# Stick-breaking attention on one core: projection groups evacuated one step later, weight splits in halves, first output halves reloaded at an earlier place, the last pair's scores two steps further ahead

## The chip, the cores and the metric

The kernel runs on one core of a Trainium2 chip. Its engines work at the same time, each through its own queue in order: TensorE (PE) multiplies, VectorE (DVE) and ScalarE (ACT) do elementwise work, GpSimd (POOL) some more of it, and SyncE (SP) issues the DMAs. They wait for one another by semaphores. The metric is the device time of one execution in microseconds (us). Before the change it is 2205.62 us, the median of three runs (2204.3 to 2206.53).

## The reference

A trunk of two layers over 1024 positions of width 1024. Layer 0 mixes by a gated linear recurrence, layer 1 by stick-breaking attention with 16 heads of width 64; each is followed by a SwiGLU network. The change touches layer 1's mixer alone:

```
qkv = hn @ w_qkv                                  # (1024, 3*1024)
z = q @ k.T / 8                                   # for each head
strict = key index < query index
log_fail = where(strict, log_sigmoid(-z), 0)
suffix = sum of log_fail over later keys
weights = where(strict, exp(log_sigmoid(z) + suffix), 0)
o = weights @ v
out = o @ w_o
```

The kernel takes no logarithms: it forms sigmoid(-z), multiplies it up from the last key to the first with a scan, and multiplies the result with sigmoid(z).

## The kernel before, in words

Each float32 operand of a large product is held as two tiles, a rounded high part and the rest, and a product is three matmuls (`mm3`, lines 140 to 143: high by high, high by low, low by high). A split is a copy on ACT (high) and a subtraction on DVE (low).

The 16 heads are worked in eight pairs. For a pair q, `qkv_steps(q)` (line 1315) projects Q, K and V (`which` = 0, 1, 2), each in two groups of 512 positions (`n`), each group in eight steps of one `mm3`. A group's sum lies in a bank of the pool `psQ` (two banks). After the eighth `mm3` the group is evacuated: DVE multiplies the bank by the row factors into `t` (line 1337). For Q and K, ACT rounds `t` (`th`, shown as `qh_`, line 1346), DVE takes the rest (`tl`, shown as `ql_`, line 1347), and SP copies both into the layouts the scores need (`move`, line 1348: four DMAs for Q, eight for K). For V, `t` is kept and `v_turn` (line 1359) transposes it on PE four steps later, through a `psQ` bank (`vt_ps`); ACT and DVE split it into `VV` (lines 1366 and 1367). At the start of each `which` the next weights are loaded and split (`next_weights`, line 1305): one ACT copy at once, two DVE halves put on the list `later`.

The attention itself has two lists. `chunks` are blocks of scores (24 in a pair: for each head eight on the diagonal and four beside it): `z_part` multiplies on PE into a bank of `psZ` (two), `z_rest` takes two sigmoids on ACT, a scan on DVE (line 1412 on the diagonal, 1414 beside it) and a product on POOL (line 1415). `units` are blocks of keys (24 in a pair): `t_part` transposes their weights on PE into `psT` (two banks), `t_split` splits them (lines 1435 and 1436), `av_part` multiplies them with V (lines 1447 and 1448). When a head's half is complete, `gather` adds its two parts (lines 1457 and 1458), and for the second head `parts` splits the result; both go through `later`. The output halves of earlier pairs are written to DRAM (`od`, lines 1469 and 1470), because the tiles `xh` and `xl` that will hold them are still the projections' input; two halves of the last pairs go straight there.

The order of PE, ACT, DVE and POOL is that of the code, written out by hand (`manual_schedule`); SP's order is left to the framework's planner. The loop over u (line 1527) interleaves: scores eight units ahead (`LEAD`), transposes two units ahead, one task of `later`, two steps of `fill`, then `av_part` of unit u. One pass of a pair is thus 24 values of u and 48 steps of `fill`. `fill` is the projection of the pair after, and behind the last one (`all_fill`, line 1490): the reloads of the output halves, two empty steps, the last `v_turn`, the release of `psQ`, a weight split, the tile `ob` in the two banks released, two empty steps more, and then 14 `mm3` of the output projection into `ob`, one in each u. The products of the second half and what follows them (`ob_ps`) belong to the next stage.

Of the kernel before, what the change touches and what calls it, by code (L numbers as in the profile page):

```python
# [19 lines left out]
ND = D // P  # L20
NT = S // P
NB = 512
NH = S // NB
# [10 lines left out]
def trunk(  # L34
# [22 lines left out]
    nc = tc.nc  # L57
    f32 = lambda t: t.bitcast(F32)
# [40 lines left out]
    xh, xl = [None] * ND, [None] * ND  # L99
# [11 lines left out]
    def load_raw(src, shape):  # L111
        raw = rp.tile([P, D], F32, tag="raw", name="raw")
        view = raw if len(shape) == 1 else raw.rearrange("p (a b) -> p a b", a=shape[0])
        nc.sync.dma_start(view, src)
        return raw
# [11 lines left out]
    def cols(w, c0, n=P):  # L127
        return w[:, c0 : c0 + n].rearrange("(k p) c -> p k c", p=P)
# [20 lines left out]
    def wtile(nm):  # L149
        return wpool[0].tile([P, D], F32R, tag="w", name=nm)  # L150
# [91 lines left out]
    half = lambda t, n: t[:, n * NB : (n + 1) * NB]  # L242
# [1021 lines left out]
    if stage == "ffn0":  # L1264
# [7 lines left out]
    NP = HEADS // 2  # L1272
# [4 lines left out]
    od = {  # L1277
        (q, n): [dp.tile([P, NB], F32, name=f"od{x}{q}_{n}") for x in "hl"]
        for n in range(NH)
        for q in range(NP)  # L1280
        if kept(q, n)
    }

    pos = ExitStack()
    with ExitStack() as st:
# [16 lines left out]

        late, later = [], []

        def next_weights(raw):
            hi, lo = wtile("whi"), wtile("wlo")
            nc.scalar.copy(hi, raw)
            for i in range(NH):
                later.append(lambda c=half(hi, i), a=half(lo, i), b=half(raw, i): nc.vector.tensor_sub(a, b, f32(c)))
            k3 = lambda t: t.rearrange("p (k c) -> p k c", k=ND)  # L1310
            return k3(hi), k3(lo)

# [2 lines left out]
        def qkv_steps(q):  # L1315
            full = lambda tag: [ap.tile([P, S], F32R, tag=tag, name=tag, bufs=4) for _ in range(2)]
            VV[q] = ap.tile([P, NT, 2, P], F32R, tag="v", name="v", bufs=2)
            for which in range(3):
                w = wq.pop((q, which))
                nx = (q, which + 1) if which < 2 else (q + 1, 0)  # L1320
                if nx[0] < NP:
                    wq[nx] = next_weights(load_raw(cols(w_qkv, nx[1] * D + nx[0] * P), (ND,)))
                else:
                    mix[0].load(0)
                    mix[0].w[mix[0].order[0]] = next_weights(mix[0].raw.pop(0))
                    mix[0].load(1)
                    mix[0].load(2)
                for n in range(NH):
                    ps = psQ.tile([P, NB], F32, tag="qk", name="qk_ps")
                    for k in range(ND):  # L1330
                        mm3(ps, w[0][:, k], w[1][:, k], xh[k][n], xl[k][n], k == 0, k == ND - 1)
                        if k == 3 and late:
                            late.pop()()
                        if k < ND - 1:
                            yield
                    t = ap.tile([P, NB], F32, tag="t", name="t", bufs=2)
                    nc.vector.tensor_mul(t, ps, rbc[n])
                    cs = slice(n * NB, (n + 1) * NB)
                    if which == 0 and n == 0:
                        Q[q] = full("q")  # L1340
                    if which == 1 and n == 0:
                        KH[q], KL[q] = full("kh"), full("kl")
                    if which < 2:
                        th = ap.tile([P, NB], F32R, tag="qh_", name="qh_", bufs=1)
                        tl = ap.tile([P, NB], F32R, tag="ql_", name="ql_", bufs=1)
                        nc.scalar.copy(th, t)
                        nc.vector.tensor_sub(tl, t, f32(th))
                        move = lambda dst, p0, src, p1: nc.sync.dma_start(f32(dst)[p0, cs], f32(src)[p1])
                        for hx, (a, b) in enumerate(((top, bot), (bot, top))):
                            if which == 0:  # L1350
                                move(Q[q][hx], a, th, a)
                                move(Q[q][hx], b, tl, a)
                            else:
                                for dst, src in ((KH[q][hx], th), (KL[q][hx], tl)):
                                    move(dst, top, src, a)
                                    move(dst, bot, src, a)
                    else:

                        def v_turn(n=n, t=t):
                            tp = psQ.tile([P, NB], F32, tag="qk", name="vt_ps")  # L1360
                            for i in range(4):
                                nc.tensor.transpose(tp[:, i * P : (i + 1) * P], t[:, i * P : (i + 1) * P], ident)
                            src = tp.rearrange("p (b h c) -> p b h c", b=4, h=2)
                            bs = slice(4 * n, 4 * n + 4)
                            for hx in range(2):
                                nc.scalar.copy(VV[q][:, bs, hx, 0:HD], src[:, :, hx])
                                nc.vector.tensor_sub(
                                    VV[q][:, bs, hx, HD:P], src[:, :, hx], f32(VV[q])[:, bs, hx, 0:HD]
                                )

                        late.append(v_turn)
                    yield


        W = {}
# [8 lines left out]
        def z_part(q, hx, j, ci, c0, c1, diag):  # L1384
            nk = (j + 1) * P
            ps = psZ.tile([P, NB], F32, tag="z", name="z_ps")
            lhsT = Q[q][hx][:, j * P : (j + 1) * P]
            nc.tensor.matmul(ps[:, 0 : c1 - c0], lhsT=lhsT, rhs=KH[q][hx][:, c0:c1], start=True, stop=False)  # L1388
            nc.tensor.matmul(ps[:, 0 : c1 - c0], lhsT=lhsT, rhs=KL[q][hx][:, c0:c1], start=False, stop=True)  # L1389
            return ps  # L1390
# [86 lines left out]
        chunks = [c for q, hx in heads for c in chunk_list(q, hx)]  # L1477
        units = [u for q, hx in heads for u in unit_list(q, hx)]
        LEAD = 8
# [10 lines left out]
        def all_fill():  # L1490
            yield from first
            for q in range(1, NP):
                yield from qkv_steps(q)
            for q, n in od:
                nc.sync.dma_start(f32(xh[q][n]), od[q, n][0])
                nc.sync.dma_start(f32(xl[q][n]), od[q, n][1])
            yield
            yield
            late.pop()()
            qs.close()  # L1500
            mix[0].proc(1)
            po = pos.enter_context(tc.tile_pool(name="fpo", bufs=1, space=PSUM, side="right", reuse_waits="tile"))
            ob = po.tile([P, S], F32, name="ob")
            mix.append(ob)
            for _ in range(2):
                yield
            for i, d in enumerate(mix[0].order[:2]):
                w = mix[0].w[d]
                for k in range(ND - 1):
                    mm3(ob[:, i * NB : (i + 1) * NB], w[0][:, k], w[1][:, k], xh[k][0], xl[k][0], k == 0, False)  # L1510
                    yield
                    yield

        fill = all_fill()
        ready = {}
        E = mybir.EngineType
        with tc.manual_schedule(engines={E.PE, E.Activation, E.DVE, E.Pool}):
            sts, first = stats_steps(), qkv_steps(0)


            for i in range(2 * ND * NH):
                if i >= 5:
                    next(sts, None)
                next(first)
                if i >= 5 and later:
                    later.pop(0)()
            for u in range(-LEAD, len(units)):
                c = u + LEAD
                if c < len(chunks):
                    z = z_part(*chunks[c])  # L1530
                if 0 <= u + 2 < len(units):
                    ready[u + 2] = t_split(t_part(*units[u + 2]), *units[u + 2])
                if c < len(chunks):
                    z_rest(z, *chunks[c])
                if later:
                    later.pop(0)()
                for _ in range(2):
                    next(fill, None)
                if u >= 0:
                    av_part(ready.pop(u), *units[u])  # L1540
            while later:
                later.pop(0)()
# [49 lines left out]
```

## Time and profile before

| | |
|---|---|
| median of three runs | 2205.62 us |
| profiled execution, whole | 2209.81 us |
| its span, first to last instruction | 2207.9 us |
| PE busy | 2176.5 us (99%) |
| DVE busy | 1709.9 us (77%) |
| ACT busy | 1150.2 us (52%) |
| POOL busy | 287.2 us (13%) |
| mean granted TensorE clock | 0.994 |

The profile is one execution. Times in its rows count from the start of the span. A row of the timeline shows start, duration, engine, source line, the operation with the tile written and the tiles read, partitions by elements, and in brackets the idle time of the engine before it with the instruction that ended it; "issue" there means that no releaser was found. Operations overlap a little, so that the start of the next one lies up to 0.1 us before the end shown. A busy PE may still run at half clock, which the column PEclk tells.

### The profile page before, as it was taken

What the parts mean: (1) busy time and instruction counts of PE and PEld (TensorE: products, weight loads), DVE (VectorE), ACT (ScalarE), POOL (GpSimd) and SP (SyncE); (2) the same over time, 40 slices, a digit from 0 to 9 for tenths busy, and PEclk for the clock granted to TensorE, in tenths of its full rate; (3) what the DMA queues carried; (4) which work ended last, traced back from release to release, by engine and by line L of the source; (5) the groups of instructions that cost most, each with busy time, mean ns of one, the idle gap of its engine ahead of it and who ended that gap; (6) DMA issues with size and microseconds to landing.
All of it is one profiled execution on the core that took longest, in us unless ns stands there. A gap on an engine that the chain in (4) does not pass through costs nothing.

```text
span 2207.9 us, 28478 instructions
## 1 busy us (share of the span) xinstructions
PE 2176.5 (99%) x10120; PEld 1805.7 (82%) x10120; DVE 1709.9 (77%) x2383; ACT 1150.2 (52%) x2007; POOL 287.2 (13%) x379
## 2 busy tenths in 40 slices
PE   7999999999999999999999999989999999999998
PEld 6888888888888888878888888878888888888887
DVE  6887778767777887878888888876876777788876
ACT  5577435343444544546666666653533444454556
POOL 2222020000000000003334333321000000000002
PEclk9999999999999999999999999989999999999999
DMA  7111412334444764444333333532133444467442
GB/s 230 48 48 39 134 39 72 102 123 158 143 149 134 261 209 122 148 136 98 89 94 96 105 87 104 177 128 70 39 110 124 148 148 133 154 225 234 137 152 86
DMA packets 298702, 277.72 MB, mean 126 GB/s; under 512 B 16312, under 2 KB 215104, under 8 KB 298560
## 3 DMA queue, kind: packets, MB, share of 16 engines
q1 hardware_dynamic: 298544, 275.91, 40.1%
q8 instruction: 79, 1.29, 0.2%
q14 instruction: 63, 0.52, 0.1%
q10 hardware_dynamic: 16, 0.00, 0.0%
HBM read 175.71 MB, written 74.97 MB: 114 GB/s over the span
## 4 chain that ended last, share of the span: by engine, by line
PE 88%; DVE 6%; ACT 3%; DMA 1%; issue 1%; SPq 1%; DVEq 0%; ACTq 0%
PE p_ps L143 18%; PE p_ps L141 18%; PE p_ps L142 18%; PE qk_ps L143 3%; PE qk_ps L141 3%; PE qk_ps L142 3%; PE wt_ps L1426 3%; PE ob_ps L142 2%; PE ob_ps L141 2%; PE ob_ps L143 2%; PE a_ps L143 2%; PE a_ps L142 2%; PE a_ps L141 2%; PE z_ps L1388 1%; DVE F L1414 1%; PE z_ps L1389 1%
## 5 line engine op out<-in xcount | busy, mean ns | idle before, releaser
L1415 POOL TENSOR_TENSOR w<-w,F 128x128 f32<-128x128 f32 (+1 forms) x192 | 183.7, 957 | 311.1 <-DVE F L1412 159.0
L143 PE MATMUL p_ps<-vh,wcl 128*128 128x512 f32 x524 | 204.2, 390 | 0.5 <-DVE wcl L682 0.5
L143 PE MATMUL p_ps<-vh,wbl 128*128 128x512 f32 x524 | 204.4, 390 | 0.3 <-DVE wbl L672 0.2
L143 PE MATMUL p_ps<-vh,wal 128*128 128x512 f32 x524 | 204.1, 389 | 0.1
L141 PE MATMUL p_ps<-vh,wbh 128*128 128x512 f32 x524 | 204.2, 390 | 0.0
L141 PE MATMUL p_ps<-vh,wch 128*128 128x512 f32 x524 | 204.1, 389 | 0.0
L142 PE MATMUL p_ps<-vl,wbh 128*128 128x512 f32 x524 | 203.9, 389 | 0.0
L142 PE MATMUL p_ps<-vl,wch 128*128 128x512 f32 x524 | 203.9, 389 | 0.0
L141 PE MATMUL p_ps<-vh,wah 128*128 128x512 f32 x524 | 203.9, 389 | 0.0
L142 PE MATMUL p_ps<-vl,wah 128*128 128x512 f32 x524 | 203.9, 389 | 0.0
L668 ACT CAST wbh<-sb 128x1024 fp32r<-128x1024 f32 (+2 forms) x69 | 69.6, 1009 | 193.7 <-DVE sb L652 193.6
L212 POOL TENSOR_TENSOR acc<-acc,rbc 128x512 f32<-128x512 f32 x30 | 40.4, 1348 | 773.6 <-ACT rbc L211 773.6
L1436 DVE TENSOR_TENSOR tl<-wt_ps,th 128x512 fp32r<-128x512 f32 x192 | 106.0, 552 | 39.2 <-ACT th L1435 37.1
L1435 ACT CAST th<-wt_ps 128x512 fp32r<-128x512 f32 x192 | 92.5, 482 | 83.1 <-PE wt_ps L1426 82.0
L141 PE MATMUL qk_ps<-vh,whi 128*128 128x512 f32 x264 | 118.6, 449 | 0.7 <-ACT vh L215 0.7
L143 PEld LDWEIGHTS p_ps<-vh,wbl 128*128 128x128 f32 x524 | 98.3, 188 | 22.3 <-DVE wbl L672 2.0
L143 PEld LDWEIGHTS p_ps<-vh,wcl 128*128 128x128 f32 x524 | 98.4, 188 | 21.9 <-DVE wcl L682 1.6
L143 PEld LDWEIGHTS p_ps<-vh,wal 128*128 128x128 f32 x524 | 98.4, 188 | 21.3 <-DVE wal L663 1.0
L142 PEld LDWEIGHTS p_ps<-vl,wah 128*128 128x128 f32 x524 | 98.4, 188 | 20.6
L142 PEld LDWEIGHTS p_ps<-vl,wch 128*128 128x128 f32 x524 | 98.4, 188 | 20.5
L142 PEld LDWEIGHTS p_ps<-vl,wbh 128*128 128x128 f32 x524 | 98.4, 188 | 20.5
L141 PEld LDWEIGHTS p_ps<-vh,wbh 128*128 128x128 f32 x524 | 98.4, 188 | 20.3 <-ACT ta L1053 0.2
(400 smaller groups left out, 5851.2 us busy)
## 6 DMA issues: line engine op xcount, KB each, us to landing
raw<-in_ffn_w_in SPq DMA_DIRECT2D x88, 512.0 KB, 3.8
vl<-pd SPq DMA_DIRECT2D x128, 256.0 KB, 3.6
pd<-U SPq DMA_DIRECT2D x90, 256.0 KB, 2.3
raw<-in_ffn_w_out SPq DMA_DIRECT2D x56, 256.0 KB, 3.9
raw<-in_attn_w_qkv SPq DMA_DIRECT2D x24, 512.0 KB, 3.8
raw<-in_lru_w_in SPq DMA_DIRECT2D x16, 512.0 KB, 4.1
acc<-pd SPq DMA_DIRECT2D x28, 256.0 KB, 2.6
pph<-rbc SPq DMA_DIRECT2D x28, 256.0 KB, 2.5
```

Of the source, the lines that this page charges most:

```text
L141: nc.tensor.matmul(ps, lhsT=wh, rhs=mh, start=first, stop=False, **kw)
L142: nc.tensor.matmul(ps, lhsT=wh, rhs=ml, start=False, stop=False, **kw)
L143: nc.tensor.matmul(ps, lhsT=wl, rhs=mh, start=False, stop=last, **kw)
L212: (eng or nc.gpsimd).tensor_add(acc[n], acc[n], sq)
L668: nc.scalar.copy(self.full(self.wb), self.full(self.sb))
L1388: nc.tensor.matmul(ps[:, 0 : c1 - c0], lhsT=lhsT, rhs=KH[q][hx][:, c0:c1], start=True, stop=False)
L1389: nc.tensor.matmul(ps[:, 0 : c1 - c0], lhsT=lhsT, rhs=KL[q][hx][:, c0:c1], start=False, stop=True)
L1414: nc.vector.tensor_tensor_scan(rev, rev, rev, first, op0=ALU.mult, op1=ALU.bypass)
L1415: nc.gpsimd.tensor_mul(wt, wt, F[:, 1 : n + 1])
L1426: nc.tensor.transpose(tp[:, c : c + P], W[q, hx, j, kb // 4][:, (kb % 4) * P : (kb % 4 + 1) * P], ident)
L1435: nc.scalar.copy(th[:, q0:], tp[:, q0:])
L1436: nc.vector.tensor_sub(tl[:, q0:], tp[:, q0:], f32(th)[:, q0:])
```

## The change

Four edits, all in the attention stage.

- A group's last step now yields before its evacuation. `t`, `th`, `tl` and the moves are issued at the beginning of the generator's next step, ahead of the next group's first `mm3`, which is in the next u. The number of steps stays.
- `next_weights` splits in halves, as three tasks of `later`: high half 0; low half 0 and high half 1; low half 1.
- The reloads are a function, `bring_back(n)`. Those of n = 0 are issued in the last pair's V projection, once its first group has been evacuated; those of n = 1 where all were before.
- Behind the last projection the two empty steps between the making of `ob` and its first `mm3` go, so that this `mm3` follows the last `v_turn` directly. In two values of u, units 2 and 6 of the last pair (`len(units) - 22` and `- 18`), one score block more is worked in place of the two steps of `fill`. From there the scores are nine, then ten units ahead.

```diff
+        def bring_back(n):
+            for q in range(NP):
+                if (q, n) in od:
+                    nc.sync.dma_start(f32(xh[q][n]), od[q, n][0])
+                    nc.sync.dma_start(f32(xl[q][n]), od[q, n][1])
+
         def next_weights(raw):
             hi, lo = wtile("whi"), wtile("wlo")
-            nc.scalar.copy(hi, raw)
-            for i in range(NH):
-                later.append(lambda c=half(hi, i), a=half(lo, i), b=half(raw, i): nc.vector.tensor_sub(a, b, f32(c)))
+            part_hi = lambda i: nc.scalar.copy(half(hi, i), half(raw, i))
+            part_lo = lambda i: nc.vector.tensor_sub(half(lo, i), half(raw, i), f32(half(hi, i)))
+
+            def second():
+                part_lo(0)
+                part_hi(1)
+
+            later.extend((lambda: part_hi(0), second, lambda: part_lo(1)))
...
                         mm3(ps, w[0][:, k], w[1][:, k], xh[k][n], xl[k][n], k == 0, k == ND - 1)
                         if k == 3 and late:
                             late.pop()()
-                        if k < ND - 1:
-                            yield
+                        yield
                     t = ap.tile([P, NB], F32, tag="t", name="t", bufs=2)
...
                         late.append(v_turn)
-                    yield
+                        if q == NP - 1 and n == 0:
+                            bring_back(0)
...
                 yield from qkv_steps(q)
-            for q, n in od:
-                nc.sync.dma_start(f32(xh[q][n]), od[q, n][0])
-                nc.sync.dma_start(f32(xl[q][n]), od[q, n][1])
+            bring_back(1)
             yield
             yield
             late.pop()()
...
             mix.append(ob)
-            for _ in range(2):
-                yield
             for i, d in enumerate(mix[0].order[:2]):
...
+            gains = [len(units) - 22, len(units) - 18]
+            c = 0
             for u in range(-LEAD, len(units)):
-                c = u + LEAD
-                if c < len(chunks):
-                    z = z_part(*chunks[c])
+                some = chunks[c : c + 1]
+                c += 1
+                for a in some:
+                    z = z_part(*a)
                 if 0 <= u + 2 < len(units):
                     ready[u + 2] = t_split(t_part(*units[u + 2]), *units[u + 2])
-                if c < len(chunks):
-                    z_rest(z, *chunks[c])
+                for a in some:
+                    z_rest(z, *a)
                 if later:
                     later.pop(0)()
-                for _ in range(2):
-                    next(fill, None)
+                if u in gains:
+                    z_rest(z_part(*chunks[c]), *chunks[c])
+                    c += 1
+                else:
+                    for _ in range(2):
+                        next(fill, None)
                 if u >= 0:
                     av_part(ready.pop(u), *units[u])
```

## The prediction

> **What bounds the kernel now.** First the stretches of the attention stage, in a table by windows (busy time of each engine with its instruction count, granted TensorE clock, DMA share, GB/s):
>
> ```profile
> core 0: us, PE busy (x) PEld busy (x) DVE busy (x) ACT busy (x) POOL busy (x), PEclk, DMA share, GB/s
> 1120.00:1180.00 60.00, 59.63 (x319) 50.06 (x318) 50.54 (x74) 39.78 (x97) 23.45 (x39) 1.00 0.36 95
> ...
> 1435.00:1440.00 5.00, 1.09 (x7) 0.75 (x7) 4.20 (x7) 3.53 (x9) 2.45 (x2) 0.89 1.06 385
> 1440.00:1445.00 5.00, 5.00 (x16) 4.12 (x17) 3.97 (x5) 3.31 (x9) 1.09 (x1) 0.50 0.80 224
> ...
> 1470.00:1475.00 5.00, 4.40 (x16) 3.70 (x17) 3.52 (x7) 1.79 (x3) 1.09 (x1) 0.50 0.00 0
> 1475.00:1480.00 5.00, 5.00 (x24) 3.94 (x23) 1.54 (x3) 1.75 (x3) 0.00 (x0) 0.85 0.00 0
> ```
>
> A head pair takes some 60 us, TensorE (PE) is busy for 59.63 of them, and VectorE (DVE) for 50.5: inside the pairs 0.37 us each is all that can be won. More lies in the last pair: PE idle after 1435, half clock after it, half clock again at 1470. The table of waits names the places (total, times, longest):
>
> ```profile
> ACT qh__9565 L1346 <- DVE t L1337: 3.3, 1, 3.3
> PE ob L141 <- issue: 3.9, 1, 3.9
> PE z_ps L1388 <- ACT w L1409: 2.2, 6, 0.4
> ```
>
> So three sums: 2.2 us (six times) where a score waits for ACT to empty its bank, which itself waited 3.3 us for `t`; 3.9 us before `ob`; and the end. The timeline shows the second (PE rows, then DVE rows; start, duration):
>
> ```profile
> 1434.00 0.60 PE L1362 MATMUL vt_ps<-ident,t 128*128 128x128 f32 x4
> 1434.36 0.42 PE L1447 MATMUL av_ps<-th,v 128*128 128x384 f32 x1
> ...
> 1435.30 0.60 PE L1426 MATMUL wt_ps<-ident,w 128*128 128x128 f32 x4
> 1439.80 0.76 PE L141 MATMUL ob<-vh,whi 128*128 128x512 f32 x1 [3.91 <-issue]
> 1440.36 0.63 PE L142 MATMUL ob<-vl,whi 128*128 128x512 f32 x1
> ...
> 1445.97 0.39 PE L142 MATMUL ob<-vl,whi 128*128 128x512 f32 x1
> ...
> 1432.86 0.67 DVE L1337 TENSOR_TENSOR t<-qk_ps,rbc 128x512 f32<-128x512 f32 x1
> 1433.63 0.42 DVE L1436 TENSOR_TENSOR tl<-wt_ps,th 128x256 fp32r<-128x256 f32 x1
> 1434.29 1.28 DVE L1414 TENSOR_TENSOR_SCAN F<-F,F 128x512 f32<-128x512 f32 x1 [0.24 <-POOL w L1415]
> 1435.61 0.69 DVE L1458 TENSOR_TENSOR oo<-av_ps,oo 64x512 f32<-64x512 f32 x1
> ...
> 1437.84 0.66 DVE L1464 TENSOR_TENSOR vl<-oo,vh 128x512 fp32r<-128x512 f32 x1
> 1438.42 0.41 DVE L1367 TENSOR_TENSOR v<-vt_ps,v 128x256 fp32r<-128x256 f32 x1
> 1439.27 0.42 DVE L1367 TENSOR_TENSOR v<-vt_ps,v 128x256 fp32r<-128x256 f32 x1 [0.44 <-ACT v L1366]
> ...
> 1441.36 0.68 DVE L1436 TENSOR_TENSOR tl<-wt_ps,th 128x512 fp32r<-128x512 f32 x1
> ```
>
> The `[...]` of the `ob` row names no releaser, but the second `v` ends at 1439.69 and `ob` starts at 1439.80: `ob` takes the two banks of the projection pool, and the last reader of those is that `v`. I read the 3.9 us as this wait, not as the reload of outputs. The whole queue of DVE from 1434.29 to 1439.69 stands before it.
>
> **The change part by part.** Below, u counts the loop's steps from the first unit of a pair.
>
> *Evacuation a step later.* No instruction is added; `t`, `th`, `tl` and the moves of each of the 48 groups go behind the next u's `tl`, scan and popped task. (1) ACT no longer sits on `qh` when the next scores arrive, so the six score waits go: -2.2 us, and a like one of 0.3 us at the stage's start. (2) The second V group's `t` now comes after `oo`; its reader is the transpose `vt_ps`:
>
> ```profile
> 1133.61 0.69 DVE L1458 TENSOR_TENSOR oo<-av_ps,oo 64x512 f32<-64x512 f32 x1
> ...
> 1134.77 0.60 PE L1362 MATMUL vt_ps<-ident,t 128*128 128x128 f32 x4
> ```
>
> `oo` frees DVE at 1134.2 (starts of such operations lie 0.6 apart), `t` ends at 1134.87, PE starts at 1134.95 in place of 1134.77: +0.18, seven times, +1.3. (3) The K halves reach the scores over SP and DMA. The first K group of a pair in before (DVE, SP, then PE; DMA issues with their KB and us to landing last):
>
> ```profile
> 1161.39 0.67 DVE L1337 TENSOR_TENSOR t<-qk_ps,rbc 128x512 f32<-128x512 f32 x1
> ...
> 1164.88 0.66 DVE L1458 TENSOR_TENSOR oo<-av_ps,oo 64x512 f32<-64x512 f32 x1
> ...
> 1163.95 1.33 SPq L1348 DMA_DIRECT2D kl<-ql__9813  x2
> ...
> 1170.75 0.28 PE L1389 MATMUL z_ps<-kl,q 128*128 128x256 f32 x1
> ...
> kl<-ql__9813 SPq DMA_DIRECT2D x4, 128.0 KB, 2.4
> ```
>
> The second `kl` move starts at 1164.7, 3.3 us after `t`, and lands near 1167.1. In the new order `t` stands behind `oo`; with ACT free that `oo` runs at about 1163.9, `t` at 1164.5, so the move lands at 1164.5 + 3.3 + 2.4 = 1170.2, and the score needs it at 1170.75: I take nothing. Bounds per pair: 0, and the 0.5 us of slack overdrawn by as much. The second K group is needed 9 us after its `t` and has more room.
>
> *Weight splits in pieces.* ACT's 1.05 us copy (128x1024) becomes two of 0.62 us (the row of `qh`, 128x512): +0.2 us on an engine idle for 20 of 60 us. The DVE halves stay, one or two u later; weights are needed 8 u after the split begins, and the raw load that their end releases, a u later, is three tiles ahead. Zero, hidden by those u; uncovered it would be one 2.5 us step per load.
>
> *Reload sooner.* SP already issues the reloads before their place in the program:
>
> ```profile
> 1413.35 0.34 SPq L1496 DMA_DIRECT2D vl<-odl  x1
> ...
> 1420.54 0.39 SPq L1470 DMA_DIRECT2D odl<-oo  x1
> 1421.03 0.41 SPq L1495 DMA_DIRECT2D vh<-odh  x1
> ...
> 1427.78 0.32 SPq L1496 DMA_DIRECT2D vl<-odl  x1
> ```
>
> The fourteen of the first half are out by 1428, land some 5 us later, 6 us before `ob`. Moved, they gain nothing. Were some issued ahead of the last pair's second K moves, SP would hold these moves: 0 to +1.5 us (three 0.5 us issues), once; I take 0.
>
> *The last pair.* (a) `t` is now at u=0 behind scan and `oo`: 1435.61 + 0.6 = 1436.2 to 1436.9. So `vt_ps` waits from 1434.0 to 1436.95. Then `tl`, scan, `vl`, `v`, `v` follow as before, 0.4 us later: `ob` at 1440.2. (b) `ob` now stands right behind `vt_ps`, so the av, score and transposes that ran from 1434.36 to 1435.66 (1.3 us) come after it, at half clock (a product that takes 0.63 us there, as at 1440.36, and 0.39 again at 1445.97; start to start 0.43 and 0.23). The two idle stretches of 2.9 us I take to lower the clock as the 3.9 us did. DVE, which got `tl` at 1441.4, gets it at 1444.5. With the extra score at u=2, whose successor must wait 0.4 us for a bank, the second `ob` step starts at 1446.0, not 1442.99: 3.0 us behind. (c) Now the tail (PE unless marked):
>
> ```profile
> 1442.99 0.78 PE L141 MATMUL ob<-xg,whi 128*128 128x512 f32 x1
> ...
> 1468.30 0.33 PE L1426 MATMUL wt_ps<-ident,w 128*128 128x128 f32 x1 [1.09 <-DVE tl L1436]
> ...
> 1470.60 1.33 PE L1426 MATMUL wt_ps<-ident,w 128*128 128x128 f32 x4 [1.62 <-DVE tl L1436]
> ...
> 1479.03 0.39 PE L141 MATMUL ob_ps<-vh,whi 128*128 128x512 f32 x1
> ...
> 1468.16 1.97 DVE L1414 TENSOR_TENSOR_SCAN F<-F,F 128x512 f32<-128x512 f32 x1
> ```
>
> From 1442.99 to 1479.03 are 36.0 us: 2.7 idle, half of the 2.5 cold us to 1445.5 (1.2), half of the 5.9 busy cold us from 1470 to 1476.5 (2.95; the clock rows, 0.50 and then 0.85 of 5 us, put the end there) and 0.3 hidden in the slow transposes leave 28.85 of work at full clock. One score (0.23) is already done in the new order: 28.6. The scans run two steps ahead of the products, so the last of them ends by about 1469 with products still to do, and the wait for it goes. I stepped the queues on from 1446.0 with the durations of such rows (0.6 a `tl`, 0.4 to 1.7 a scan, 0.5 an ACT copy). What is late next: the score at u=7 waits 1.2 us for its bank (two scores went at u=6, and ACT reads each with two passes of 0.5), and the transposes at u=16 find PE ready at 1468.2 and their bank free at 1469.6, when the `tl` behind the last scan ends: 1.4. 1446.0 + 28.6 + 2.6 = 1477.2, against 1479.03: -1.8 us. Bounds: without any of these idle times -4.4; with half clock once more (2.95) +1.1.
>
> Sum: -0.3 - 2.2 + 1.3 - 1.8 = -3.0 us. Of the profiled execution (span 2207.9, whole time 2209.81) that makes 2206.8; it stood 4.2 us above the median 2205.62, so the forecast for the median is 2202.6, 0.14% less. About 0.2% (4.4 us) is what a measurement of this kernel tells from no change: this counts as the same.
>
> **Rules against the trace.** The rows show half clock after one idle stretch of 3.91 us, and again after two of 1.09 and 1.62 us with work between. [...]
>
> **Rivals.** *The clock holds:* both new gaps are shorter than the 3.9 us one. Then the 5.3 us from 1440.2 to 1445.5 are not halved: -2.7 more, -5.7, 2199.9. Against it stands 1470. [...] *The tail runs full:* the bank and `tl` waits (2.6) do not appear, since the scans came early: -5.6, 2200.0; for it, DVE's queue then holds less; against it, DVE is the full engine from 1460 on. Both together: -8.3, 2197.3. *Slower, the K halves come late:* each pair's first score with new keys waits. My 0.5 us of slack rests on DVE's new order; if `t` slips behind a further `tl` and scan (0.33 + 1.28) the wait is 1.1 us in each of seven pairs, +7.7: 2210.3. It decides from a wait of 1.06 us on (3.0 + 4.4 over seven); at 0.4 us the sum is zero. For it: the chain is on four engines in order, against it, the copy that ACT no longer blocks. *No effect:* the bubble costs what the lead earns (half clock in the tail too): 0, 2205.6.
>
> **How the numbers follow.** The forecast 0.42, clock holds 0.13, tail full 0.13, slower 0.20, no effect 0.12. Of the forecast's 0.42, its own range (-5 to 0) puts 0.05 beyond -4.4, and of the slower case 0.03 lies within 0.2%, of no effect 0.06 beyond +0.2%: faster 0.31, same 0.46, slower 0.23. The 8 in 10 reach from both gains together, less a little (-9), to a K wait of 0.9 us (+3.3): 2196.6 to 2208.9.
>
> **What would show it.** Right: the PE wait of scores on ACT gone from the six pairs; a PE wait before `vt_ps` of 0.1 to 0.3 us in each pair and of 3 us in the last; `ob` starting with 3 us of wait behind a second `v`; no PE wait above 1 us near the last scan; half clock around the first `ob`. Wrong: PE waits before L1389 (K late), a clock of 1.00 around `ob`, idle before `ob` that ends with a landing DMA, or a tail that goes to half clock again. The forecast fails most easily in the term -1.8, a difference between 3.0 lost and 4.8 won.

## The result and the profile after

The changed kernel takes 2211.76 us (median; 2209.74 to 2214.94) against 2206.13 us for the kernel before on the same chip (2204.3 to 2208.31). The ratio is 1.0025, 95% interval 1.0014 to 1.0036: slower by 5.6 us, where 3 us less were forecast, and above the range. The interval lies above 1, but not wholly above the 0.2% from which the forecast counts a change. Its profiled execution took 2214.94 us with a span of 2213.1.

For a single execution the span is a poor measure: the code ahead of the stage is the same in both kernels, and yet the stage's first score came anywhere from 991.1 to 994.5 in the profiles below. All kernels are therefore compared by two stretches inside the stage: the *six pairs*, from the last `vt_ps` of the first pair to that of the seventh, and the *end*, from there to the first `ob_ps`. First the rows of before that bound them, then those of after (PE rows of the timeline):

```profile
1014.59 0.60 PE L1362 MATMUL vt_ps<-ident,t 128*128 128x128 f32 x4
...
1376.38 0.60 PE L1362 MATMUL vt_ps<-ident,t 128*128 128x128 f32 x4
```

```profile
1011.91 0.60 PE L1372 MATMUL vt_ps<-ident,t 128*128 128x128 f32 x4
...
1380.46 0.66 PE L1372 MATMUL vt_ps<-ident,t 128*128 128x128 f32 x4
...
1482.94 0.40 PE L141 MATMUL ob_ps<-vh,whi 128*128 128x512 f32 x1
```

Before (its `ob_ps` row, 1479.03, stands in the prediction): 361.8 and 102.65. After: 368.55 and 102.5. The loss lies in the pairs. PE's waits there (table of waits of after: us in total, times, longest):

```profile
PE vt_ps L1372 <- DVE t L1347: 3.2, 3, 2.9
PE ob L141 <- issue: 2.6, 1, 2.6
PE z_ps L1399 <- DMA kh<-qh__12230: 1.8, 1, 1.8
PE z_ps L1399 <- ACT w L1420: 1.7, 2, 1.2
PE wt_ps L1437 <- DVE tl L1447: 1.1, 2, 0.7
PE z_ps L1400 <- DMA kl<-ql__9211: 0.6, 1, 0.6
PE z_ps L1400 <- DMA kl<-ql__10721: 0.6, 1, 0.6
```

The six waits on ACT `w` are gone, as forecast; the two left belong to the last pair. New are waits for `kl`, the moved half of K, of 0.5 to 0.6 us, one in each of the seven pairs (two are listed here). How one comes about (after; DVE, POOL, SP and PE rows):

```profile
1232.08 1.31 DVE L1423 TENSOR_TENSOR_SCAN F<-F,unit 128x128 f32<-128x128 f32 x1
1233.43 0.69 DVE L1469 TENSOR_TENSOR oo<-av_ps,oo 64x512 f32<-64x512 f32 x1
1234.13 0.69 DVE L1347 TENSOR_TENSOR t<-qk_ps,rbc 128x512 f32<-128x512 f32 x1
1235.52 0.69 DVE L1357 TENSOR_TENSOR ql__10721<-t,qh__10720 128x512 fp32r<-128x512 f32 x1 [0.69 <-ACT qh__10720 L1356]
...
1232.02 1.10 POOL L1426 TENSOR_TENSOR w<-w,F 128x512 f32<-128x512 f32 x1 [1.25 <-DVE F L1425]
...
1236.71 1.18 SPq L1358 DMA_DIRECT2D kl<-ql__10721  x2
...
1239.77 0.36 PE L1400 MATMUL z_ps<-kl,q 128*128 128x256 f32 x1 [0.61 <-DMA kl<-ql__10721]
```

This is the second K group of a pair. From `t` at 1234.13 to the product that uses the half are 5.6 us of chain: ACT, DVE, SP, landing. Before, the same operations stood so (DVE, then PE):

```profile
1171.92 0.66 DVE L1337 TENSOR_TENSOR t<-qk_ps,rbc 128x512 f32<-128x512 f32 x1
...
1180.06 0.28 PE L1389 MATMUL z_ps<-kl,q 128*128 128x256 f32 x1
```

There the chain had 8.1 us, 2.5 to spare. Against the pair's `vt_ps` (1134.77 before, 1194.40 after) `t` moved from 37.15 to 39.73: 2.6 us later. That takes the whole room, and the scores come a little earlier in the pair besides.

### The profile page after: what moved, and what is told of

Same layout as the page of the kernel before. It is cut to its first block, busy times and chain, and to the rows that moved or that the text cites. A ratio compares the mean times of both kernels' runs of the same rounds, so it can differ in the third digit from the quotient of the medians.

```text
span 2213.1 us, 28506 instructions
## 1 busy us (share of the span) xinstructions
PE 2174.9 (98%) x10120; PEld 1802.8 (81%) x10120; DVE 1728.4 (78%) x2383; ACT 1152.4 (52%) x2031; POOL 288.8 (13%) x379
## 3 DMA queue, kind: packets, MB, share of 16 engines
q8 instruction: 80, 1.31, 0.2%
## 4 chain that ended last, share of the span: by engine, by line
PE 84%; DVE 8%; ACT 3%; DMA 2%; issue 1%; SPq 1%; DVEq 0%; ACTq 0%
PE p_ps L143 18%; PE p_ps L141 18%; PE p_ps L142 18%; PE ob_ps L141 2%; PE ob_ps L142 2%; PE ob_ps L143 2%; PE qk_ps L143 2%; PE qk_ps L141 2%; PE qk_ps L142 2%; PE a_ps L143 2%; PE a_ps L142 2%; PE a_ps L141 2%; PE wt_ps L1437 2%; DVE F L1425 2%; PE z_ps L1400 1%
## 5 line engine op out<-in xcount | busy, mean ns | idle before, releaser
L1423 DVE TENSOR_TENSOR_SCAN F<-F,unit 128x128 f32<-128x128 f32 (+3 forms) x128 | 128.5, 1004 | 4.4 <-ACT F L1419 4.3
```

The source lines that it names most:

```text
L1423: nc.vector.tensor_tensor_scan(rev, rev, unit[:, NB - n :][:, ::-1], first, op0=ALU.mult, op1=ALU.add)
```

## The experiments

Theory: the late evacuation of K costs the time. Rival: the last pair's new order costs it. In the table, "six pairs" and "end" are worked out from the same three rows of each profile; the ratio is to the kernel before, timed beside it. The six pairs of before agree in both profiles, while its two ends lie 2 us apart: the end of a single profile can be off by as much.

| kernel | median us | ratio (95%) | six pairs | end |
|---|---|---|---|---|
| before, two profiles | 2206.13 | | 361.8, 361.8 | 102.65, 100.6 |
| after, five profiles | 2211.76 | 1.0025 (1.0014 to 1.0036) | 368.55, 365.2, 366.2, 365.2, 366.0 | 102.5 in all |
| evacuation alone | 2215.93 | 1.0037 (1.0024 to 1.0049) | 370.4 | 101.4 |
| change without it | 2202.53 | 0.9976 (0.9966 to 0.9987) | 357.9 | 101.3 |
| last pair's order alone | 2207.19 | 1.0001 (0.9992 to 1.0010) | 361.8 | 101.9 |
| splits alone | 2202.74 | 0.9983 (0.9975 to 0.9992) | 357.8 | 102.2 |
| change, K at once | 2205.24 | 0.9995 (0.9986 to 1.0003) | 359.9 | 103.4 |
| change, V at once | 2209.39 | 1.0016 (1.0007 to 1.0025) | 363.0 | 102.3 |
| change, fill first | 2205.12 | 0.9993 (0.9984 to 1.0002) | 359.1 | 101.05 |
| change, no POOL product | 2204.03, one run | | 359.9 | 100.15 |
| without it, V turn early | 2199.72 | 0.9971 (0.9960 to 0.9982) | 357.8 | 98.5 |
| the same, `ob` later | 2200.29 | 0.9974 (0.9964 to 0.9984) | 357.8 | 98.7 |

**The changed kernel again.** No edit.

> The changed kernel once more, nothing edited. In its first profile the 6.0 us of the span fall into: seven pairs with a wait of 0.5 to 0.6 us for the second half of K (about +0.5 us a pair over before, +3.3 by 1315), 3.5 us more in the seventh pair, where the move of the second half of K ran 2.95 us instead of 1.18, and the rest about zero. If that stretched move is a chance of one execution, the seventh pair takes 60.9 us here, not 64.3, and the span is 2209 to 2210. If it belongs to the program, the seventh pair takes 64 us again and the span is 2213. The K waits of 0.5 to 0.6 us are there in both cases.

Median 2212.79, ratio 1.0020 (1.0011 to 1.0029). The seventh pair took 60.9 us, not 64.3, and the K waits were there. So 3.4 us of the first profile came and went with one SP move; the rest stayed.

**One part alone.** The evacuation a step later, on the kernel before:

```diff
-                        if k < ND - 1:
-                            yield
+                        yield
                     t = ap.tile([P, NB], F32, tag="t", name="t", bufs=2)
...
                         late.append(v_turn)
-                    yield
```

> The kernel before with one part of the change: the projected groups evacuated a step later. Weight splits, reloads and the last pair stay as before. Theory (the evacuation costs): K waits of 0.5 to 0.6 us in each of the seven pairs as in the changed kernel, the score waits of 0.37 gone, vt waits of 0.2 to 0.3; pairs of 60.8 to 60.9 against 60.40, and some 2.9 us of a vt wait in the last pair; span 2210 to 2214, that is +2 to +6 on before. Rival (the last pair's new order costs): without it this kernel keeps before's time or better, 2204 to 2208, with pairs of at most 60.4.

And all of the change but this:

```diff
-                        yield
+                        if k < ND - 1:
+                            yield
...
                             bring_back(0)
+                    yield
```

> The changed kernel with the projected groups evacuated at once, as before; the weight splits, the reloads and the last pair stay changed. Theory (the evacuation costs): no K waits, pairs of 60.4, no vt wait of 2.9 in the last pair, and the tail of 41.6 us from the last projection to ob against 45.0 kept; span 2201 to 2205, that is -3 to -7 on before. Rival (the last pair's new order costs): 2208 or more. Weight splits in pieces, if they cost anything, show as pairs over 60.45.

And the last pair's order alone, on the kernel before:

```diff
             mix.append(ob)
-            for _ in range(2):
-                yield
...
+            gains = [len(units) - 22, len(units) - 18]
...
+                if u in gains:
+                    z_rest(z_part(*chunks[c]), *chunks[c])
+                    c += 1
```

> The kernel before with one part of the change: the last pair's scores two steps further ahead (two score blocks issued in place of fill steps, the two empty steps taken out). Theory: everything up to the last pair as before, the last pair faster by 2 to 4.8 us, span 2203 to 2206. It differs from the changed kernel without the late evacuation only by splits and reloads: if these are free, both have the same span within 0.5. Rival (the last pair's new order costs): 2208 or more.

The evacuation alone is slower than the whole change, and the change without it faster than before: the theory holds on the whole. Two things went against what I expected. First, with the evacuation alone the score waits on ACT did not go; they grew. The table of waits, then ACT and PE rows of that kernel:

```profile
PE z_ps L1386 <- ACT w L1407: 6.0, 6, 1.1
```

```profile
1237.28 0.62 ACT L1345 CAST qh__10706<-t 128x512 fp32r<-128x512 f32 x1 [3.74 <-DVE t L1336]
1237.81 1.04 ACT L1307 CAST whi<-raw 128x1024 fp32r<-128x1024 f32 x1
...
1239.62 0.50 PE L1386 MATMUL z_ps<-kh,q 128*128 128x512 f32 x1 [1.10 <-ACT w L1407]
```

The evacuation has been moved right in front of the whole-tile copy of weights, and ACT does both before it empties the next score's bank. The K waits, expected in every pair, are absent but for two, of 0.2 and 1.2 us. So this kernel is slow by the evacuation, but by another path than the changed one; that K is the path in the changed kernel rests on the experiments below. Second, the last pair's order alone is worth nothing that the times show (2207.19 against 2207.75 beside it), so the other 4.7 us between it and the change without the evacuation must come from splits or reloads, or from several parts together.

**Splits alone**, on the kernel before:

```diff
-            nc.scalar.copy(hi, raw)
-            for i in range(NH):
-                later.append(lambda c=half(hi, i), a=half(lo, i), b=half(raw, i): nc.vector.tensor_sub(a, b, f32(c)))
...
+            later.extend((lambda: part_hi(0), second, lambda: part_lo(1)))
```

> The kernel before with one part of the change: the weight splits in pieces. The changed kernel with the old evacuation has pairs of 59.65 us, the kernel before and the one with the new last pair alone 60.40; the two differ in splits and reloads. If the splits make the 0.75 us, this kernel has pairs of 59.65, no wait of scores for ACT, and a span 4.5 to 5.3 us shorter than before, 2202 to 2204. If the reloads or the two together do it, the pairs stay at 60.40 and the time at 2206 to 2208.

Six pairs of 357.8: all of it. (The reloads begin later, ahead of the eighth `vt_ps`. From the seventh to the eighth take 57.08 us here and in the change without the evacuation, and in both SP issues the first reload 36.43 us behind the seventh: moved in the code, the reloads come no earlier, and up to there they cost nothing.) PE no longer waits for ACT, and the reason is in DVE's queue. First before, then this kernel:

```profile
1142.82 0.66 DVE L1309 TENSOR_TENSOR wlo<-raw,whi 128x512 fp32r<-128x512 f32 x1
1143.40 0.68 DVE L1337 TENSOR_TENSOR t<-qk_ps,rbc 128x512 f32<-128x512 f32 x1
```

```profile
1138.64 0.66 DVE L1308 TENSOR_TENSOR wlo<-raw,whi 128x512 fp32r<-128x512 f32 x1
1139.22 0.68 DVE L1342 TENSOR_TENSOR t<-qk_ps,rbc 128x512 f32<-128x512 f32 x1
1140.59 0.69 DVE L1352 TENSOR_TENSOR ql__9575<-t,qh__9574 128x512 fp32r<-128x512 f32 x1 [0.69 <-ACT qh__9574 L1351]
...
1141.86 0.67 DVE L1308 TENSOR_TENSOR wlo<-raw,whi 128x512 fp32r<-128x512 f32 x1
```

Before, both low halves stand ahead of `t`; now the second stands behind it, a step later. Against the pair's `vt_ps` (1134.77 and 1131.43) `t` begins at 8.63 before and at 7.79 here. ACT, which waits for `t`, is free 0.84 us sooner, and the score wait of 0.37 is covered.

**Which group is late, and why.** The changed kernel with the K groups evacuated at once:

```diff
-                        yield
+                        if k < ND - 1 or not (which == 1):
+                            yield
...
+                    if which == 1:
+                        yield
```

> The changed kernel with the groups of K alone evacuated at once; those of Q and V stay a step later. Theory (the second half of K comes late because its evacuation moved): no wait of scores for K, pairs 0.7 to 0.8 us shorter than the 60.85 of the changed kernel, 60.1; the waits of vt_ps for t (0.15 to 0.31 and 2.9 in the last pair) stay. Seven pairs: 5 us off the changed kernel, 2206 to 2208. Rival (the queue of DVE is too long whatever group goes first): the wait moves to another operand and the pairs stay at 60.6 or more, 2211 or more.

The same edit with `which == 2`, the V groups:

> The changed kernel with the groups of V alone evacuated at once. Theory: the vt waits go (0.31 a pair, and 2.9 in the last pair, of which the ob wait takes back some 2.6, as where all groups go at once), the K waits of 0.5 to 0.6 stay, pairs of 60.4 to 60.55, last pair about 57.3 and the tail 44.2: together 2 to 3 us off the changed kernel, 2208 to 2210. Rival (vt waits are only the other side of the K waits): pairs stay at 60.85.

K at once takes 5.3 us off the six pairs (365.2 to 359.9), 0.88 a pair, and the waits for `kl` are gone (its long end has half clock for 13.6 us in one stretch, where the changed kernel has 6.8); V at once takes 2.2 off (0.37 a pair), and the K waits stay. Both rivals fall: the wait doesn't wander, and the two add up (5.3 + 2.2 against 365.2 - 357.9 = 7.3).

The changed kernel with `fill` ahead of the list `later`:

```diff
-                if later:
-                    later.pop(0)()
                 if u in gains:
...
                         next(fill, None)
+                if later:
+                    later.pop(0)()
```

> The changed kernel with one order turned round: within a step u the two steps of fill (and with them the late evacuation) come before the task of the list later (an oo, a low half of weights), not behind it. All evacuations stay a step late. Theory (t of K is late by its step and by the oo before it): t of the second K group comes 0.7 us earlier, the K waits of 0.5 to 0.6 fall to 0.1 or go, the vt waits of 0.15 to 0.31 go, pairs of 59.8 to 60.2, span 3 to 6 us shorter than the changed kernel's 2208.5 to 2213. Rival (only the step itself counts, 2.5 us): K waits stay at 0.5 and pairs at 60.8.

`t` now stands in front of `oo`; it begins 38.83 us behind the pair's `vt_ps` (1193.74), 0.9 sooner than after, and the K waits are gone (DVE rows of this kernel):

```profile
1231.35 1.30 DVE L1423 TENSOR_TENSOR_SCAN F<-F,unit 128x128 f32<-128x128 f32 x1
1232.57 0.66 DVE L1347 TENSOR_TENSOR t<-qk_ps,rbc 128x512 f32<-128x512 f32 x1
1233.92 0.69 DVE L1357 TENSOR_TENSOR ql__10719<-t,qh__10718 128x512 fp32r<-128x512 f32 x1 [0.69 <-ACT qh__10718 L1356]
1234.64 0.69 DVE L1469 TENSOR_TENSOR oo<-av_ps,oo 64x512 f32<-64x512 f32 x1
```

The six pairs fell by 6.1 us; the median fell with them, to a ratio to before whose interval includes 1. (The edit moves all that is on the list `later`, not `oo` alone.)

The changed kernel without POOL's product beside the diagonal:

```diff
-            nc.gpsimd.tensor_mul(wt, wt, F[:, 1 : n + 1])
+            if diag:
+                nc.gpsimd.tensor_mul(wt, wt, F[:, 1 : n + 1])
```

> The changed kernel without the product of weights and F on POOL for the score blocks beside the diagonal (so the weights of those blocks lack this factor); all else stays. Theory (the scans before the evacuation of K are held up by POOL's products): the 128x128 scan after the blocks beside the diagonal takes 0.4 us and not 1.3, the 128x512 scans 1.0 to 1.3 and not 1.8 to 2.0, t of the second K group comes 0.9 us or more earlier in the pair, and the wait of scores for K goes or falls below 0.2; pairs of at most 60.2. Rival (the step and the oo alone make K late): scans as before, K waits of 0.5 to 0.6 stay.

In groups by line and shape (DVE scans of 1010 to 1425; busy, mean ns), first after, then this kernel:

```profile
L1423 DVE TENSOR_TENSOR_SCAN F<-F,unit 128x128 f32<-128x128 f32 x27 | 26.8, 994 | 0.0
```

```profile
L1423 DVE TENSOR_TENSOR_SCAN F<-F,unit 128x128 f32<-128x128 f32 x28 | 14.9, 531 | 0.0
```

The mean scan of 128x128 falls from 0.99 to 0.53 us, `t` comes 37.86 us behind `vt_ps` instead of 39.73, and the K waits go. So three things make the half late: the step itself, the `oo` ahead of it, and scans held up by POOL. Taking away either of the last two is enough.

**The last pair.** The change without the late evacuation, and `v_turn` issued two fill steps earlier:

```diff
             bring_back(1)
+            late.pop()()
             yield
             yield
-            late.pop()()
             qs.close()
```

> Meant to be the best: the changed kernel with the old evacuation, and the last pair's second turn of V issued two fill steps earlier, ahead of one more scan and vl on DVE; the first product into ob stays where it was. If ob waits for the v subtractions behind DVE's queue, the wait of 5.2 us before ob falls to 2 to 3 us and the span ends 1.5 to 3 us earlier than without this edit: 2199 to 2201. If ob waits for something else (a reload that lands, the release of the pool), the wait stays 5.2 less nothing and the time 2202.5.

The end shrinks from 101.3 to 98.5. Up to 1.7 us of that may be the clock's: half clock lasts 3.4 us in this profile and 6.8 in the other. By the medians, each against the kernel before timed beside it, this kernel gains 6.5 us and the one without the edit 5.2, and their intervals overlap. It beats the kernel before and the changed one. DVE and PE rows:

```profile
1429.45 0.42 DVE L1378 TENSOR_TENSOR v<-vt_ps,v 128x256 fp32r<-128x256 f32 x1
1430.31 0.43 DVE L1378 TENSOR_TENSOR v<-vt_ps,v 128x256 fp32r<-128x256 f32 x1 [0.44 <-ACT v L1377]
...
1430.84 0.47 PE L141 MATMUL ob<-vh,whi 128*128 128x512 f32 x1 [2.45 <-issue]
```

`ob` again starts 0.1 us behind the end of the second `v`, now that this `v` comes earlier: the reading of the row without a releaser is borne out.

The same kernel with two more empty steps of u before `ob`'s first product:

```diff
             late.pop()()
             yield
             yield
+            yield
+            yield
             qs.close()
```

> The kernel with the early V turn (2199.7) with the first product into ob moved two steps of u back, behind two more scores and two more blocks of transposes, so that TensorE has work while the v subtractions run. If the wait before ob is what costs there (2.45 us and some 3 us at half clock, 4 us in all), no wait above 1.5 us stands between the last projection and ob, the granted clock stays at 1.00 or falls for less than 2 us, and the time is 2196.5 to 2198.5. If VectorE's queue sets the end of the last pair, the waits only move towards its end and the time stays within 1 us of 2199.7.

Here the rival was right: within 0.6 us. PE's waits moved from `ob` to the scores' banks, with 3.4 us of half clock behind them as in the kernel above (PE rows):

```profile
1432.39 0.50 PE L1401 MATMUL z_ps<-kh,q 128*128 128x512 f32 x1 [1.94 <-ACT w L1422]
...
1434.45 0.58 PE L1401 MATMUL z_ps<-kh,q 128*128 128x256 f32 x1 [1.10 <-ACT w L1422]
...
1435.54 0.78 PE L141 MATMUL ob<-vh,whi 128*128 128x512 f32 x1
```

**How much comes and goes.** Three more executions of the changed kernel and one of the kernel before, no edits.

> The changed kernel, one more look. In the first of its two profiles SP's move of the second half of K took 2.95 us in the seventh pair and cost 3.5 us; in the second it did not. If such a stretch comes and goes, one or two of three more looks show it, in whichever pair, and the stage from the first pair to ob_ps takes 467.7 us without it and 471 with it. If the first profile was a lone chance, all three take 467.7.

> As for the look before this one: 467.7 us for the stage without a stretched move, 471 with one.

> As for the two looks before this one: 467.7 us for the stage without a stretched move, 471 with one.

> The kernel before, one look. Its first score of the stage came at 994.28 in its first profile and at 991.5 to 994.5 in the twelve of other kernels, whose code ahead of the stage is the same. If this is chance, it may come anywhere in that range here, and the stage takes 464.4 us again; if the kernel before is slower ahead of the stage, it comes at 994 again.

Their times are 2211.47, 2212.86, 2211.38 and 2206.59. A stretched move cost time in three of the five profiles of the changed kernel, each time at the same move of the seventh pair. SP and PE rows of the first profile, then the SP rows of two of these executions:

```profile
1358.47 2.95 SPq L1358 DMA_DIRECT2D kl<-ql__12231  x2
...
1362.51 0.36 PE L1399 MATMUL z_ps<-kh,q 128*128 128x256 f32 x1 [1.76 <-DMA kh<-qh__12230]
```

```profile
1358.04 2.19 SPq L1358 DMA_DIRECT2D kl<-ql__12231  x2
```

```profile
1358.52 2.04 SPq L1358 DMA_DIRECT2D kl<-ql__12231  x2
```

It cost 3.4, 1.0 and 0.8 us. Two more, in the sixth pair (2.02 us beside the stretch of 2.19, and 2.41 for moves of `kh` in the execution of 2212.86), cost nothing. So the stage takes 467.6 to 467.7 us without one at that move, as expected, and 468.5 to 471 with one, by how far it is stretched; I had expected 471 each time. Two things were settled beside it. The mean of the stage (six pairs and end) over five profiles is 468.7 us, 366.2 + 102.5; over the two of before it is 463.4. The difference of 5.3 answers to the 5.6 us by the medians. And the first score of the kernel before came at 993.15, not at 994.28 as in its first profile: chance.

## Why the prediction was wrong

The sign of the sum failed, and with it the range. By its steps:

*Evacuation, (3): the K halves, taken as nothing.* This is the step that failed. I worked out the slack of the first K group with care and let the second off with "is needed 9 us after its t and has more room". The rows give 8.1 us, and the step moved `t` itself by 2.6 us, which I did not take off; the chain needs 5.6. The half comes 0.5 to 0.6 us late, and that costs 0.88 us a pair. The rival "the K halves come late" named the mechanism and its queue (a further `tl` and scan); it put the wait at 1.1 us for a chance of 0.20. That its 2210.3 comes near the measured time is in part luck: it keeps the -3.0 of the sum, which did not come so, and sets 1.1 us a pair against the 0.88 measured.

*Evacuation, (1): the score waits go, -2.2.* They went, but not by this edit: alone it leaves 6.0 us of them, and the splits in pieces take them away. The size was off as well: I multiplied the 0.37 us listed by six. Pairs with such a wait (five of the six) take 60.40 us, and 59.65 in the kernel with the splits alone, so each was worth 0.75. The listed idle is counted from the modelled end of the product before, and products normally overlap (in before the one of 0.39 us at 1179.26 has the next at 1179.49); at the spot the start-to-start excess is 0.54. (The wait of 0.58 for `kl` likewise costs 0.79 at the spot.) What makes the rest of the 0.75 I have not followed.

*Evacuation, (2): +0.18 seven times for `vt_ps`.* Right in kind, half the size: 0.37 a pair by the kernel with V at once.

*Weight splits, zero.* Wrong: -4.0 us over the six pairs, by what stands in front of `t` on DVE. I had priced the added ACT time, and not the order that the three tasks give to DVE's queue.

*Reload, zero.* Right as far as the eighth `vt_ps` (57.08 us with and without the edit); behind it no run has the reloads alone.

*The last pair, -1.8.* The new end has the shape that was worked out: `vt_ps` waits 2.9 us, `ob` starts behind the second `v`, half clock around it, a score wait of 1.2 us, no second half-clocked place at the end. Its rows in after:

```profile
1441.32 0.66 PE L1372 MATMUL vt_ps<-ident,t 128*128 128x128 f32 x4 [2.91 <-DVE t L1347]
1444.53 0.77 PE L141 MATMUL ob<-vh,whi 128*128 128x512 f32 x1 [2.56 <-issue]
```

and its windows (the clock is the third figure from the end):

```profile
1440.00:1445.00 5.00, 1.12 (x5) 0.92 (x6) 4.01 (x8) 3.07 (x6) 2.44 (x2) 0.79 1.05 385
1445.00:1450.00 5.00, 4.78 (x15) 3.70 (x14) 1.97 (x3) 1.41 (x4) 0.00 (x0) 0.53 0.80 216
```

Its length is not that of the sum: from the last `vt_ps` to `ob_ps` it took 41.6 us in all five profiles, and 1477.2 - 1436.95 are 40.25. Of the 1.4 us missing, 0.5 lie ahead of the second step of `ob` (at 1450.89, 9.6 us behind `vt_ps`, where the sum has 9.05). Behind it PE waits a little less than I allowed (2.3 us for 2.6), so the work itself, 28.6 us in the sum, was put about 1.2 too low; where, is open.

Nor was the old end what I took it for. Of its 45.0 us from the last `vt_ps` to `ob_ps`, the second execution of the kernel before needed only 43.0 (1432.92 to 1475.89), with the same waits and less half clock (its windows):

```profile
1437.00:1442.00 5.00, 3.28 (x11) 2.72 (x12) 4.04 (x6) 2.88 (x6) 1.36 (x1) 0.66 0.93 291
1442.00:1447.00 5.00, 5.00 (x32) 4.46 (x31) 4.31 (x8) 3.71 (x12) 2.81 (x4) 1.00 0.29 84
...
1467.00:1472.00 5.00, 3.48 (x15) 3.07 (x16) 3.98 (x7) 1.79 (x3) 1.09 (x1) 0.72 0.00 0
1472.00:1477.00 5.00, 5.00 (x25) 3.90 (x25) 1.79 (x4) 1.75 (x3) 0.00 (x0) 0.94 0.00 0
```

The rows of the profile on which I forecast that belong beside those of the prediction:

```profile
1445.00:1450.00 5.00, 5.00 (x28) 4.48 (x28) 3.43 (x7) 2.87 (x9) 2.26 (x6) 0.92 0.00 0
...
1465.00:1470.00 5.00, 2.89 (x17) 1.90 (x15) 5.00 (x5) 3.26 (x9) 2.18 (x2) 0.97 0.00 0
```

In windows of half a us the clock of that profile reads 0.50 from 1439 to 1445.5, and 1.00 up to 1438.5 and from 1446 on; so I take a clock of 0.66 over 5 us as half clock for 3.4 of them. Counted so, half clock held for 3.4 us at each of the two places in the second execution, and for 6.8 to 6.9 at each in the first (5.9 of them busy at the end). I took half of the 5.9 as a fixed price and counted it as won. Against the mean of the two ends of before (101.6) the new end of 102.5 loses 0.9 us, 0.8 of which may be its K wait, instead of winning 1.8.

So the six pairs go 361.8 - 4.0 (splits) + 5.3 (K) + 2.2 (V) = 365.3, against 365.2 in the profiles without a stretched move; about 1 us on the mean comes from the stretched moves, and 0.9 from the end. With K at once the change is level with the kernel before (0.9995): what the K halves cost is what made it slower.

Rivals: the clock did not hold (0.79 and 0.53 in the windows of after above), and the tail was not full; "no effect" is what the last pair's order alone gave.

## What to carry to other kernels

A step that moves an operation moves the start of every chain behind it: write for each consumer the time from the operation to its need, take off the move, and compare with the chain's length, for every group and not for the one that looks tightest. Price a wait by the distance between two periodic marks with and without it; idle time times count came out at half here. Before a half-clocked stretch of one profile enters a sum, see it in a second one.

## What the runs showed of the hardware

A scan on DVE that began while a product of POOL ran took longer. The 128x128 scan that began at 1232.08, just behind a product of 1.10 us begun at 1232.02, took 1.31 us, of which 1.04 pass until the product ends; at the same place of the kernel without that product it takes 0.42. In after, 28 of the 29 such scans between 1000 and 1440 begin inside a product that has 0.31 to 1.04 us left; they take 0.60 to 1.31, and each ends 0.27 to 0.29 us behind the product. The one that begins where no product is running takes 0.41, as do all 28 of before, none of which begins inside one (0.41 to 0.42). Why, no run shows.

Half clock came after gaps of 1.9 us and less too, and lasted unequally. In the last kernel of the table it followed gaps of 1.94 and 1.10 us (0.78 us for the first product into `ob`, which took 0.47 in the kernel above it). Two waits near the end of the kernel before, of 1.09 and 1.62 us, were followed by 6.8 us of half clock in one execution and by 3.4 in another (rows above). Summed from adjoining windows of 5 us in nine profiles (both of before, two of after, and the evacuation taken out, splits alone, K at once and the last two kernels of the table), the half clock behind 1425 lasted 3.4 to 3.5 us at four places, 6.8 to 6.9 at seven, and 13.6 at one. What sets these lengths no run shows.

In all five executions of the changed kernel SP took 0.9 to 1.8 us longer than usual at the moves of the seventh pair's second K group or soon after, but not at the same instruction: three times in the moves of `kl` (2.04 to 2.95 us for a pair that takes 1.18), and in the other two some moves later, where nothing waits for it (one of 0.38 us took 1.50 and 1.31). Between 1358 and 1361 the DMA view shows one packet of the instruction queue in each of the three profiles with a stretched move of `kl`, and none in the other two. First that of after (packets, MB, share), then the late stop of one execution:

```profile
q8 instruction: 1, 0.02, 3.7%
```

```profile
1363.09 1.50 SPq L1481 DMA_DIRECT2D odl<-oo  x1
```

After has 18 such packets between 1010 and 1440; at three of them SP takes longer than usual (here, at 1241.18 with 1.73 us for an issue of 0.38, and at 1434.48 with 1.11 for one of 0.41), at fifteen it does not. What held SP no run shows.
